# Loading and storing the first sixteen tokens of each partition in pieces of 1, 1, 2, 4 and 8

## The chip, the cores and the metric

The kernel runs on one core of one Trainium2 chip. The metric is the device time of one execution in microseconds. Six executions of the kernel before took 241.51 to 243.63 us, with a median of 242.13 us. One of them was recorded by the hardware profiler; all rows of a profile shown here come from such a recorded execution.

## The reference

The kernel is the dispatch step of a mixture of experts: each token's vector is written out once for each of its two experts, scaled by that expert's weight.

```
x:              16 x 1024 x 512   float32   (16384 tokens of 2 KB)
expert_weights: 16 x 1024 x 2     float32
out = x[:, :, None, :].repeat(2, axis=2) * expert_weights[..., None]
                16 x 1024 x 2 x 512 float32 (16384 tokens of 4 KB)
```

`expert_indices` is an input, but no value of it enters the result. So 33.6 MB of x are read, 0.13 MB of weights, and 67.1 MB are written; each element of x is multiplied twice.

## The kernel before

The 16384 tokens are laid over the 128 partitions of the on-chip memory so that partition p holds tokens 128p to 128p + 127. A partition's 128 tokens lie together in x (256 KB) and in the output (512 KB). `A_TOTAL` (line 25) is this 128. In what follows "16 tokens" always means 16 tokens of each partition.

The weights are loaded whole by one transfer on SyncE's (SP's) queue, line 45, into `w_tile`: 1 KB per partition. A loop of eight steps (line 47) then takes `TX = 16` tokens at a time. Line 49 loads them by one transfer on ScalarE's (ACT's) queue: 32 KB per partition, 4 MB in all. The pool of these tiles has two buffers, so loads 0 and 1 can be issued at once, and load 2 waits until VectorE is done with all of tile 0.

Within a step, an inner loop of two takes `TO = 8` tokens at a time. For each token and each of the two experts, VectorE (DVE) runs one multiply of 128 x 512 elements by a value per partition (line 59), 16 for an output tile. When the 16 are done, line 67 stores the tile by one transfer on SP's queue: again 32 KB per partition, 4 MB. The pool of output tiles has four buffers, so VectorE can be four tiles ahead of the stores at most, and its first multiply into a fifth waits for the first store to have landed.

Nothing plans or reorders this: each engine runs its instructions in the order written. ACT's queue holds only the eight loads, SP's the weights' load and the sixteen stores, VectorE's the 256 multiplies. The transfers of both queues run on the same 16 DMA engines. In the trace each transfer of a 128-partition tile is 128 packets, one per partition, eight on each engine; the packets of x and of the output are all 32 KB.

Of the kernel before, what the change touches and what calls it, by code (L numbers as in the profile page):

```python
# [1 line left out]

# [4 lines left out]


@with_exitstack
def kernel(  # L10
    ctx: ExitStack,
    tc: tile.TileContext,
    x: bass.AP,
    expert_indices: bass.AP,
    expert_weights: bass.AP,
    out: bass.AP,
):
    nc = tc.nc

    batch, seq, hidden = x.shape  # L20
    k = expert_weights.shape[-1]
    P = nc.NUM_PARTITIONS
    ntok = batch * seq
    assert ntok % P == 0
    A_TOTAL = ntok // P

    xr = x.rearrange("b s h -> (b s) h").rearrange("(p a) h -> p (a h)", a=A_TOTAL)
    outr = out.rearrange("b s k h -> (b s) (k h)").rearrange(
        "(p a) n -> p (a n)", a=A_TOTAL
    )  # L30
    wr = expert_weights.rearrange("b s k -> (b s) k").rearrange(
        "(p a) k -> p (a k)", a=A_TOTAL
    )
    f32 = mybir.dt.float32
    row = k * hidden

    TX = 16
    TO = 8

    w_pool = ctx.enter_context(tc.tile_pool(name="w_pool", bufs=1))  # L40
    x_pool = ctx.enter_context(tc.tile_pool(name="x_pool", bufs=2))
    o_pool = ctx.enter_context(tc.tile_pool(name="o_pool", bufs=4))

    w_tile = w_pool.tile([P, A_TOTAL * k], f32)
    nc.sync.dma_start(out=w_tile, in_=wr)

    for i in range(A_TOTAL // TX):
        x_tile = x_pool.tile([P, TX * hidden], f32)
        nc.scalar.dma_start(
            out=x_tile, in_=xr[:, i * TX * hidden : (i + 1) * TX * hidden]  # L50
        )
        for j in range(TX // TO):
            o_tile = o_pool.tile([P, TO * row], f32)
            for t in range(TO):
                at = (j * TO + t) * hidden
                for kk in range(k):
                    c = (i * TX + j * TO + t) * k + kk
                    o = t * row + kk * hidden
                    nc.vector.tensor_scalar(  # L59
                        out=o_tile[:, o : o + hidden],  # L60
                        in0=x_tile[:, at : at + hidden],
                        scalar1=w_tile[:, c : c + 1],
                        scalar2=None,
                        op0=mybir.AluOpType.mult,
                    )
            first = (i * TX + j * TO) * row
            nc.sync.dma_start(out=outr[:, first : first + TO * row], in_=o_tile)


# [1 line left out]
_INS = ['x', 'expert_indices', 'expert_weights']  # L71
_OUTS = [((16, 1024, 2, 512), 'float32')]


# [23 lines left out]
```

## Time and profile before

| what | value |
|---|---|
| median of six executions | 242.13 us |
| the profiled execution, its own time | 243.63 us |
| its span, first to last recorded event | 241.8 us |
| VectorE busy | 102.4 us (42%), 256 multiplies |
| read from and written to HBM | 33.69 MB and 67.11 MB, 417 GB/s over the span |
| stores: issue to landing, median of 16 | 44.9 us |
| loads of x: issue to landing, median of 8 | 24.6 us |
| load of the weights: issue to landing | 10.5 us |
| first multiply starts | 13.67 us |
| first store issued | 20.13 us |

Times within an execution count from the start of the span. The rows of digits divide the span into 40 equal slices of 6.05 us; a digit is the busy share of a slice in tenths, 9 standing for 90% or more. The row "DMA" is the mean busy share of the 16 DMA engines, the row below it what they moved. The queue named q1 is SP's and q10 is ACT's. Where the profile speaks of a releaser it means the event that ended a wait.

### The profile page before, as it was taken

How to read it: one execution, taken by the hardware profiler on the slowest of the kernel's cores; microseconds unless marked ns; L12 is line 12 of the kernel's file. 1: busy time of each engine (PE TensorE's matmuls, PEld its weight loads, DVE VectorE, ACT ScalarE, POOL GpSimd, SP SyncE). 2: the span in 40 equal slices, each digit the busy share in tenths (PEclk: the TensorE clock that was granted, in tenths of full speed). 3: DMA queues.
4: the chain of work that ended last, by engine and by line, in shares of the span. 5: the costliest groups of instructions: out<-in, count | busy, mean ns of one | idle time of the engine just before them, and what ended most of it. 6: DMA issues, size and time to landing. Idle time of an engine off the chain costs nothing.

```text
span 241.8 us, 358 instructions
## 1 busy us (share of the span) xinstructions
DVE 102.4 (42%) x256; POOL 0.2 (0%) x4
## 2 busy tenths in 40 slices
DVE  0079994039800904582073640649009295500000
POOL 0000000000000000000000000000000000000000
DMA  6999999999999999999999999999999999999993
GB/s 274 442 434 423 434 348 423 434 428 417 434 434 412 434 434 434 434 423 434 401 428 434 417 434 434 430 434 428 434 428 428 434 434 434 434 434 434 434 434 152
DMA packets 3602, 100.81 MB, mean 417 GB/s; under 512 B 400, under 2 KB 528, under 8 KB 528
## 3 DMA queue, kind: packets, MB, share of 16 engines
q1 hardware_dynamic: 2448, 67.24, 64.6%
q10 hardware_dynamic: 1152, 33.55, 33.4%
q14 instruction: 2, 0.02, 0.0%
HBM read 33.69 MB, written 67.11 MB: 417 GB/s over the span
## 4 chain that ended last, share of the span: by engine, by line
DMA 52%; DVE 21%; another core or an unknown queue 13%; issue 0%; DVEq 0%
DMA out_dram<-o_tile 36%; DVE o_tile L59 21%; DMA x_tile<-in_x_dram 16%; DVEq L93 0%; DVEq L59 0%
## 5 line engine op out<-in xcount | busy, mean ns | idle before, releaser
L59 DVE TENSOR_SCALAR o_tile<-x_tile,w_tile 128x512 f32<-128x512 f32 x256 | 102.4, 481 | 106.4 <-DMA out_dram<-o_tile 75.8
L82 POOL MEMSET const-bfloat16-1.0<- 128x1 bf16 x1 | 0.1, 102 | 0.0
L82 POOL MEMSET const-uint8-127<- 128x1 uint8 x1 | 0.1, 102 | 0.0
L82 POOL MEMSET const-float32-0.0<- 128x1 f32 x1 | 0.1, 99 | 0.2 <-issue 0.2
L82 POOL MEMSET const-float32-1.0<- 128x1 f32 x1 | 0.1, 99 | 0.0
## 6 DMA issues: line engine op xcount, KB each, us to landing
out_dram<-o_tile SPq DMA_DIRECT2D x16, 4096.0 KB, 44.9
x_tile<-in_x_dram ACTq DMA_DIRECT2D x8, 4096.0 KB, 24.6
w_tile<-in_expert_weights_dram SPq DMA_DIRECT2D x1, 128.0 KB, 10.5
```

Source lines behind the costliest of these rows:

```text
L59: nc.vector.tensor_scalar(out=o_tile[:, o : o + hidden], in0=x_tile[:, at : at + hidden], scalar1=w_tile[:, c : c + 1], scalar2=None, op0= ...
L82: nc = _bacc.Bacc("TRN2", target_bir_lowering=False, num_devices=1)
```

## The change

The first entry of a list of pieces, `[1, 1, 2, 4, 8]`, describes the first 16 tokens, and seven entries `[16]` describe the rest. A tile of x is loaded by one transfer per piece, and a store is issued whenever a piece ends or eight tokens are complete. So load 0 becomes five transfers, of 2, 2, 4, 8 and 16 KB per partition, all into one tile of x. The first output tile, tokens 0 to 7, leaves in four transfers, of 4, 4, 8 and 16 KB per partition; tokens 8 to 15 leave in one as before. Loads 1 to 7 and stores 1 to 15 keep their sizes, and so do the pools, the weights' load and the layout of tokens over partitions; the list `groups` has one group, which holds all 128 tokens of a partition. ACT's queue then has 12 loads, SP's the weights and 19 stores, VectorE the same 256 multiplies in the same order.

```diff
+    groups = [[[1, 1, 2, 4, 8], [16], [16], [16], [16], [16], [16], [16]]]
...
-    nc.sync.dma_start(out=w_tile, in_=wr)
+    def rows(of_all, done, T):
+        return of_all[done * P : (done + T) * P, :].rearrange(
+            "(p a) n -> p (a n)", a=T
+        )
...
+        nc.sync.dma_start(
+            out=w_tile[:, done * k : (done + T) * k], in_=rows(wf, done, T)
+        )
...
-        nc.scalar.dma_start(
-            out=x_tile, in_=xr[:, i * TX * hidden : (i + 1) * TX * hidden]
+        for pieces in group:
+            x_tile = x_pool.tile([P, TX * hidden], f32)
+            at = 0
+            for n in pieces:
+                nc.scalar.dma_start(
+                    out=x_tile[:, at * hidden : (at + n) * hidden],
+                    in_=xr[:, (a0 + at) * hidden : (a0 + at + n) * hidden],
+                )
+                at += n
+            ends = [sum(pieces[: i + 1]) for i in range(len(pieces))]
+            first = 0
+            for t in range(at):
+                if t % TO == 0:
+                    o_tile = o_pool.tile([P, TO * row], f32)
                 for kk in range(k):
-                    c = (i * TX + j * TO + t) * k + kk
-                    o = t * row + kk * hidden
+                    c = (done + a0 + t) * k + kk
+                    o = t % TO * row + kk * hidden
                     nc.vector.tensor_scalar(
...
-            first = (i * TX + j * TO) * row
-            nc.sync.dma_start(out=outr[:, first : first + TO * row], in_=o_tile)
+                if t + 1 in ends or (t + 1) % TO == 0:
+                    nc.sync.dma_start(
+                        out=outr[:, (a0 + first) * row : (a0 + t + 1) * row],
+                        in_=o_tile[:, first % TO * row : (t % TO + 1) * row],
+                    )
+                    first = t + 1
```

More of the change, by code (lines that the diff above doesn't have):

```diff
@@ L25 @@
     A_TOTAL = ntok // P
[L27 to L33, printed above, removed]
     f32 = mybir.dt.float32
@@ L38 @@
     TO = 8
+    groups = [[[1, 1, 2, 4, 8], [16], [16], [16], [16], [16], [16], [16]]]
+    assert sum(sum(sum(t) for t in g) for g in groups) == A_TOTAL
+    xf = x.rearrange("b s h -> (b s) h")
+    of = out.rearrange("b s k h -> (b s) (k h)")
+    wf = expert_weights.rearrange("b s k -> (b s) k")
     w_pool = ctx.enter_context(tc.tile_pool(name="w_pool", bufs=1))
@@ L44 @@
     w_tile = w_pool.tile([P, A_TOTAL * k], f32)
-    nc.sync.dma_start(out=w_tile, in_=wr)
-    for i in range(A_TOTAL // TX):
-        x_tile = x_pool.tile([P, TX * hidden], f32)
-        nc.scalar.dma_start(
-            out=x_tile, in_=xr[:, i * TX * hidden : (i + 1) * TX * hidden]
-        )
[L52 to L55, printed above, removed]
+    def rows(of_all, done, T):
+        return of_all[done * P : (done + T) * P, :].rearrange(
+            "(p a) n -> p (a n)", a=T
+        )
+    done = 0
+    for group in groups:
+        T = sum(sum(t) for t in group)
+        nc.sync.dma_start(
+            out=w_tile[:, done * k : (done + T) * k], in_=rows(wf, done, T)
+        )
+        done += T
+    done = 0
+    for group in groups:
+        T = sum(sum(t) for t in group)
+        xr = rows(xf, done, T)
+        outr = rows(of, done, T)
+        a0 = 0
+        for pieces in group:
[12 more added lines that the diff above has]
+                    o_tile = o_pool.tile([P, TO * row], f32)
                 for kk in range(k):
-                    c = (i * TX + j * TO + t) * k + kk
-                    o = t * row + kk * hidden
+                    c = (done + a0 + t) * k + kk
+                    o = t % TO * row + kk * hidden
                     nc.vector.tensor_scalar(
                         out=o_tile[:, o : o + hidden],
-                        in0=x_tile[:, at : at + hidden],
+                        in0=x_tile[:, t * hidden : (t + 1) * hidden],
                         scalar1=w_tile[:, c : c + 1],
@@ L65 @@
                     )
-            first = (i * TX + j * TO) * row
-            nc.sync.dma_start(out=outr[:, first : first + TO * row], in_=o_tile)
+                if t + 1 in ends or (t + 1) % TO == 0:
[4 more added lines that the diff above has]
+                    first = t + 1
+            a0 += at
+        done += T
 _INS = ['x', 'expert_indices', 'expert_weights']
```

## The prediction

> **What bounds the kernel now.** I read the page from the top: the busy shares and the 40 slices first, because they say which resource is never free, then the DMA queues, the chain of waits, and last a table of short windows around the stretch that the change touches.
>
> ```profile
> span 241.8 us, 358 instructions
> ...
> DVE 102.4 (42%) x256; POOL 0.2 (0%) x4
> ...
> DVE  0079994039800904582073640649009295500000
> ...
> DMA  6999999999999999999999999999999999999993
> GB/s 274 442 434 423 434 348 423 434 428 417 434 434 412 434 434 434 434 423 434 401 428 434 417 434 434 430 434 428 434 428 428 434 434 434 434 434 434 434 434 152
> ...
> q1 hardware_dynamic: 2448, 67.24, 64.6%
> q10 hardware_dynamic: 1152, 33.55, 33.4%
> ...
> HBM read 33.69 MB, written 67.11 MB: 417 GB/s over the span
> ```
>
> The DMA row is 9 in every slice but the first and the last: the 16 DMA engines have work from about 2 us to about 238 us. The queues of the stores (q1, with the weights) and of the loads (q10) take 64.6 + 33.4 = 98.0% of the engines' time. VectorE is busy for 42% and idles most of the rest. In the undisturbed slices the rate is 434 GB/s; 100.81 MB at that rate need 232.3 us, and the span is 241.8 us. So 9.5 us at most are there to be won by anything that doesn't cut bytes. They are made of: the head, about 2 us before data flows (packet records begin at 1.1 to 2.1 us, engine by engine); the end, about 4 us (the window 236 to 238 us still has a DMA share of 0.76, 238 to 240 us has 0.15, and the span runs to 241.8); and some 3.5 us in slices under 434, of which one slice, the sixth (30.2 to 36.3 us) at 348 GB/s, alone is 6.05 x (1 - 348/434) = 1.2 us.
>
> The chain of waits agrees: its greatest part is the store, its second VectorE waiting in turn for a buffer that a store must free.
>
> ```profile
> DMA 52%; DVE 21%; another core or an unknown queue 13%; issue 0%; DVEq 0%
> DMA out_dram<-o_tile 36%; DVE o_tile L59 21%; DMA x_tile<-in_x_dram 16%; DVEq L93 0%; DVEq L59 0%
> ```
>
> The table of waits gives us in total, times and longest:
>
> ```profile
> DVE o_tile L59 <- DMA out_dram<-o_tile: 75.8, 9, 12.7
> DVE o_tile L59 <- DMA x_tile<-in_x_dram: 27.2, 2, 13.7
> ```
>
> The 21% of VectorE in the chain does not set the end: while those multiplies run, the DMA row stays 9. The 13.7 us that VectorE waits for the first load look like the place where the change helps. Whether they do depends on what the DMA engines have to do meanwhile: columns here are the window's length, VectorE, GpSimd, PEclk, the DMA share and GB/s.
>
> ```profile
> 14.00:16.00 2.00, 2.00 (x6) 0.00 (x0) 1.00 0.87 377
> 16.00:18.00 2.00, 2.00 (x6) 0.00 (x0) 1.00 1.02 442
> 18.00:20.00 2.00, 2.00 (x6) 0.00 (x0) 1.00 1.14 492
> 20.00:22.00 2.00, 2.00 (x7) 0.00 (x0) 1.00 0.79 328
> 22.00:24.00 2.00, 2.00 (x7) 0.00 (x0) 1.00 1.07 459
> 24.00:26.00 2.00, 2.00 (x7) 0.00 (x0) 1.00 1.10 475
> ```
>
> A packet of 1.2 us is booked whole in one window, so single rows swing around 1; the six average 1.00. There is no gap between the loads and the first store. The two x buffers let loads 0 and 1 be issued at 0.73 us together; by the completion records load 1 leaves the engines at 21.3 to 22.8 us; the first store is issued at 20.13 us, so its packets are there in time. The DMA engines never waited for stores to begin.
>
> **The change, part by part.** Removed: no byte and no multiply.[...]
>
> Added on ACT's queue: 4 more loads. A load takes 366 ns there (the median of the eight). Load 1, the one behind them, is issued at 0.73 + 5 x 0.37 = 2.6 us in place of 1.1 us. By then the engines hold 4 MB of pieces, 9.7 us of work, which covers it. Without that cover it would cost 1.5 us. Piece 1 is 0.26 MB, 0.6 us of transfer, more than the 0.37 us until piece 2 is issued, so the queue does not run dry between pieces either.
>
> Added on SP's queue: 3 more stores at 333 ns each. SP has nothing between 1.1 and 20.1 us, so they cost nothing there.
>
> Added to the DMA engines: packets. The records show one packet per partition and transfer, 8 on each engine, plus one completion record of 9 ns. Loads: 4 x 8 = 32 more per engine; stores: the first 8-token store becomes four, 3 x 8 = 24 more. The 32 KB packets take 1213 ns (27.0 bytes a ns). No packet of 2, 4, 8 or 16 KB from the kernel is in the trace; the nearest below is the weights' 1 KB packet, median 46 ns, where 27 bytes a ns would make 38: 8 ns for being a packet. Its mean of 53 ns gives 15 ns. So 56 x 8 = 0.45 us on each engine, at most 56 x 15 = 0.84; I take 0.45, since the dear ones are the very first, and 7 x 9 ns = 0.06 us for completions. This falls on engines that are busy to the end, nothing hides it: **+0.5 us**.
>
> Here a rule of the Trainium skill speaks much louder against the change: DMA: Bandwidth & Descriptors, section "Bandwidth", asks for transfers of 1 MiB and more for 75% of peak, and its fit gives about 2.0 us fixed per DMA. By it 7 more DMAs cost 14 us and the kernel would take 256 us. The row says otherwise for DMAs that stand in a queue: between 212 and 236 us only stores run, several transfers one after the other, at a share of 100.5% and 434 GB/s. The fixed time is in the landing of each, and other packets fill it. I use the row, 0.5 us.
>
> Moved: VectorE's first multiply. It waits for piece 1 and the weights. The weights landed after 10.5 us because each of their 8 packets per engine alternated with one of 1213 ns; now they alternate with small ones, and both are through about 1 us after data begins to flow, near 4 us with the landing. At 399 ns a multiply (12.77 us for 32) store 1 is issued near 5.5 us in place of 20.1. The new waits on VectorE (one per piece in place of one) hold up its next multiplies, and through them SP's stores and ACT's load 2. The last piece of 8 tokens lands after 4.2 MB of loads and some 2 MB of stores, at about 15 us; its 16 multiplies end near 22 us, against 26.4 before. So load 2 comes some 4 us sooner, and nothing is later. None of it shortens the end, since the engines that carry it are full: by 22 us they have moved 8.7 MB out of 12.7 MB issued by then.
>
> Moved too: stores now run beside loads 0 and 1. Reads stretch when stores run beside them: q10's 33.4% is 80.8 us for 64 packets per engine, 77.6 us at 1213 ns, so 3.1 us lost, of which the packet records put only 0.2 us in the first two loads, which ran alone. That is 0.5 us for each of the six mixed loads. After the change about 1.2 loads more are mixed: 0.6 us, if the stretching goes by load; below nothing if it belongs to load 2's start alone (the 348 slice). Between 0.6 and -1.2 I take +0.3, nearer the mean row, since five other loads show some of it.
>
> Sum: 0.45 + 0.06 + 0.3 = 0.8 us. On the profiled execution, 243.63 us with a span of 241.8 and 1.8 us around it, that gives a span of 242.6 and 244.4 us. That execution is the longest of the six; on the median, 242.13, it gives **242.9 us**, +0.3%. A measurement of this kernel can tell about 0.5% (1.2 us) from no change, so I forecast no change that can be told.
>
> **The rivals.** (1) Slower: small packets are dearer than the weights' packet says. The weights' packets alternated with large ones; in the first 3 us after the change all packets on an engine are 1 to 4 KB, in step over 16 engines, at a row pitch of 256 KB. If packets of 2 and 4 KB move at half the rate, 1 MB of loads takes 2.4 us more; less what stores fill, 1.5. With 0.8 from packets and 0.6 from mixing the time is about 244.5 to 245. It decides from 0.7 us of such loss on. For it: the very first 32 KB reads took up to 1.76 us and one 1 KB packet 0.34 us. Against it: once flowing, the 1 KB packets held 46 ns steadily.
> (2) Faster: the 1.2 us lost in the sixth slice come from load 2's abrupt meeting with the first stores, and go when the two meet gradually; and the uneven end (share 0.76, then 0.15) happens to close up by a us. 242.1 + 0.5 - 1.2 - 1 = 240.4. Against it: loads 3 to 7 met stores that were already flowing, and still stretched.
> (3) The forecast that the words of the change suggest: stores begin 14 us sooner and so the end comes sooner, toward 228 us. The bytes exclude it: 232.3 us at 434 GB/s, before head and end.
> (4) The packets' cost vanishes among the ends of the engines, which differ by 2 us: 242.1.
>
> **How the numbers follow.** My sum 0.46, (4) 0.10: together 0.56 within 0.5% (240.9 to 243.3). (1) 0.32, all above 243.3. (2) 0.12, below 240.9, (3) under 0.01 in it. The range reaches from 241.2, which holds all but the lowest of (2), to 245.0, the upper end of (1).
>
> **What would show it.** Right: the DMA row still 9 from the second slice on; packets 896 more and 112 completion records, 4610 in all; the first store issued near 5.5 us; load 2 near 22 us; VectorE's wait for loads about as long in sum but in pieces, its wait for stores longer; the span within 1 us of 242.6. Wrong: a slice of the first 12 us clearly under 400 GB/s (rival 1), or the sixth at 434 and the last emptier (rival 2). A DMA digit under 9 in the middle would overthrow the bound on which all of this stands.

## The result: 0.2% faster, and the profile after

The changed kernel's median is 241.91 us (35 executions, 241.28 to 244.02), the kernel before has 242.53 us beside it (72 executions, 241.16 to 244.53). The ratio is 0.9979, 95% interval 0.9965 to 0.9993. So the change gains about 0.5 us. I had forecast 0.8 us of loss. Both are under the 0.5% that I had called the limit, and 241.91 lies in the range; but the sign was wrong, and the interval excludes no change. (A later, smaller comparison, e9_after_again below, has 0.9984 with an interval that just includes it.) The quickest executions of the two kernels are alike, 241.28 and 241.16 us. What differs is how many are quick: 23 of 35 are under 242.2 us after the change, 15 of 72 before.

The traced execution took 242.26 us, with a span of 240.5. These are the lines of its page that answer to those shown of before: the span, the slices, the packets and the queues.

```profile
span 240.5 us, 372 instructions
...
DVE  2558398460276404673054910917207495500000
...
DMA  6999999999999999999999999999999999999994
GB/s 190 401 458 412 447 435 406 458 431 436 431 431 420 425 431 436 436 425 431 436 431 436 431 436 425 432 431 431 431 431 436 436 431 436 431 431 436 436 425 185
DMA packets 4610, 100.81 MB, mean 419 GB/s; under 512 B 512, under 2 KB 640, under 8 KB 1280
...
q1 hardware_dynamic: 2880, 67.24, 65.1%
q10 hardware_dynamic: 1728, 33.56, 33.2%
```

The DMA row is still 9 in every slice but the first and the last, so the bound is what it was, and VectorE's row shows the early work (digits 2 and 5 in the first slices, where it had 0). The GB/s row holds the answer. The first slice fell from 274 to 190 and the second from 442 to 401; the sixth rose from 348 to 435. Slices are 6.0 us, so the first two lost (84 + 41) x 6.0 = 0.75 MB, 1.7 us at 434 GB/s, and the sixth regained 87 x 6.0 = 0.52 MB, 1.2 us. The rest is spread over the other slices: slices 7 to 39 have 430 GB/s on average before and 432 after.

The table of waits of the changed kernel, in us, times and longest:

```profile
DVE o_tile L83 <- DMA out_dram<-o_tile: 85.8, 11, 12.7
DVE o_tile L83 <- DMA x_tile<-in_x_dram: 15.1, 5, 5.0
DVE o_tile L83 <- issue: 3.8, 1, 3.8
```

VectorE waits 12 us less for loads (27.2 before) and 10 us more for stores (75.8): what it gains at the start it gives back to buffers that full DMA engines free no sooner.

**Where the time went, in the packet records.** In the kernel's transfers a packet of a given size has a steady time, its median; what single packets take above it I call stretching, summed and divided by the 16 engines. "Price" is all packets and completion records at their medians. The last store leaves a completion record on each engine; their mean is when the DMA engines are done on average, and the lag is how far the slowest is behind that. Times in this table, and wherever a mean end is given, put the first packet at 1.1 us; the profile's windows put it at 1.7 us, so these times are 0.6 us early against the windows. Two traces of each kernel (the second ones are the runs e1_before_again and e9_after_again below):

| trace, us per engine | price | stretching 0-8 us | 8-40 us | after 40 us | mean end | lag | span |
|---|---|---|---|---|---|---|---|
| before | 233.49 | 0.20 | 1.49 | 1.68 | 237.9 | 2.2 | 241.8 |
| before, second | 233.49 | 0.44 | 1.60 | 1.30 | 237.6 | 2.6 | 241.9 |
| changed | 234.02 | 1.58 | 0.04 | 0.64 | 236.9 | 1.7 | 240.5 |
| changed, second | 234.02 | 1.45 | 0.03 | 0.81 | 236.9 | 2.2 | 240.9 |

The packets cost 0.53 us more. The stretching falls from 3.35 to 2.28 us: 1.2 us more in the first 8 us, 1.5 less up to 40 us, 0.8 less after. Sum: -0.55 us. The mean end moved by 0.85, so 0.3 us (gaps of engines that start late, records that overlap by 3 to 4 ns) is not separated by this account. The lag is 0.45 us smaller. Together that is 1.3 us, which fits the spans (1.2 us) but is twice the difference of the medians: both traces of before are of executions from the upper part of its range (243.63 and 243.72 us), those of the changed kernel less so (242.26 and 242.66 us).

### The profile page after: what moved, and what is told of

Its sections match the earlier page's. It is cut to its first block, busy times and chain, and to the rows that moved or that the text cites. A ratio compares the mean times of both kernels' runs of the same rounds, so it can differ in the third digit from the quotient of the medians.

```text
span 240.5 us, 372 instructions
## 1 busy us (share of the span) xinstructions
DVE 102.9 (43%) x256; POOL 0.2 (0%) x4
## 2 busy tenths in 40 slices
DMA packets 4610, 100.81 MB, mean 419 GB/s; under 512 B 512, under 2 KB 640, under 8 KB 1280
## 4 chain that ended last, share of the span: by engine, by line
DMA 43%; DVE 23%; another core or an unknown queue 18%; issue 2%; DVEq 0%; ACTq 0%
DMA out_dram<-o_tile 32%; DVE o_tile L83 23%; DMA x_tile<-in_x_dram 11%; DVEq L123 0%; ACTq L70 0%; DVEq L83 0%
## 6 DMA issues: line engine op xcount, KB each, us to landing
out_dram<-o_tile SPq DMA_DIRECT2D x2, 512.0 KB, 16.4
```

## The experiments

Two theories stood at first. **M (meeting)**: before loses its 3 us because load 2 and the first stores start into each other, and an early store takes that away. **C (chance)**: the stretching comes and goes by itself. Before's own code ran again first; the other kernels are the changed one with a list of load pieces and a list of store pieces per tile that can differ:

```diff
-    groups = [[[1, 1, 2, 4, 8], [16], [16], [16], [16], [16], [16], [16]]]
-    assert sum(sum(sum(t) for t in g) for g in groups) == A_TOTAL
+    loads = ...
+    stores = ...
+    groups = [loads]
+    cuts = iter(stores)
...
-            ends = [sum(pieces[: i + 1]) for i in range(len(pieces))]
+            cut = next(cuts)
+            ends = [sum(cut[: i + 1]) for i in range(len(cut))]
```

### The kernel before, again

No edit.

> The kernel before, once more, timed against itself: it gives the error of a ratio and a second trace. Theory M (meeting): before loses about 2.9 us per engine to stretched 32 KB packets because load 2 and the first stores start into each other; the stretching is a property of the kernel, so the second trace again has 2.5 to 3.5 us of it and a slice under 400 GB/s between 24 and 40 us. Theory C (chance): the stretching comes and goes from execution to execution; the second trace has anything from 0.5 to 3 us, and no slice need be low. Both: ratio 1.000, interval within 0.998 to 1.002.

Median 242.56 us against 242.71, ratio 0.9991 (0.9963 to 1.0019). The stretching was 3.34 us in place of 3.37, in the same places. The transfers of the window from 26 to 38 us, first in the trace of before, then in this one (kind: packets, MB, share of 16 engines):

```profile
DMA packets 155, 4.56 MB, mean 380 GB/s; under 512 B 15, under 2 KB 15, under 8 KB 15
...
q1 hardware_dynamic: 106, 2.98, 59.3%
q10 hardware_dynamic: 48, 1.57, 40.3%
```

```profile
DMA packets 156, 4.56 MB, mean 380 GB/s; under 512 B 16, under 2 KB 16, under 8 KB 16
...
q1 hardware_dynamic: 105, 2.92, 59.2%
q10 hardware_dynamic: 50, 1.64, 41.3%
```

40.3% of 12 us on 16 engines is 77.4 us for 48 read packets, 1.61 us each where 1.21 is the steady time; 41.3% for 50 gives 1.59. Two traces with the same stretching in the same places speak against C: it seems to belong to the kernel. But they are only two, and both of long executions, so they do not exclude C. The same window of the changed kernel, in both its traces:

```profile
DMA packets 292, 5.36 MB, mean 446 GB/s; under 512 B 32, under 2 KB 32, under 8 KB 34
```

```profile
DMA packets 288, 5.30 MB, mean 441 GB/s; under 512 B 27, under 2 KB 27, under 8 KB 30
```

The 380 GB/s of before are 446 and 441 there (over 434, since a packet is booked whole where it starts).

### One part of the change at a time

Only the loads cut, then only the stores:

```diff
+    loads = [[1, 1, 2, 4, 8], [16], [16], [16], [16], [16], [16], [16]]
+    stores = [[8, 8], [8, 8], [8, 8], [8, 8], [8, 8], [8, 8], [8, 8], [8, 8]]
```

> Only the first load is cut in 1, 1, 2, 4, 8; the stores stay at 8 tokens. The first store is issued near 11 to 14 us, while load 1 is under way. M: the stretching later on goes (-2.4 us), the slow start of the small load packets stays (+1.6), packets +0.3: -0.5 us, ratio 0.998, as in the changed kernel. C: the later stretching is unrelated, slow start and packets alone: +0.3 to +1.9 us, ratio 1.001 to 1.008.

```diff
+    loads = [[16], [16], [16], [16], [16], [16], [16], [16]]
+    stores = [[1, 1, 2, 4, 8], [8, 8], [8, 8], [8, 8], [8, 8], [8, 8], [8, 8], [8, 8]]
```

> Only the first stores are cut in 1, 1, 2, 4, 8; load 0 is one transfer of 16 tokens. The first store is issued near 14.5 us in place of 20.1. M: no slow start, the later stretching goes: -2.4 + 0.2 = -2.2 us, ratio 0.991. C: +0.2 us for packets, ratio 1.001.

Loads cut: median 244.31 us, ratio 1.0066 (1.0042 to 1.0090). Stores cut: 243.20, ratio 1.0014 (0.9995 to 1.0032). M had put them at 0.998 and 0.991; both fit what C had put (1.001 to 1.008, and 1.001). Neither half of the change gains; only the two together do. With the stores cut, the stretching that should have gone had moved: none in load 2, but 1.18 us in load 1, at 19 to 22 us, while the first small stores run beside it. So cutting the stores does not make the meeting gentle. (The profile's windows put this at 19 to 23 us.)

### The first load in two halves

```diff
+    loads = [[8, 8], [16], [16], [16], [16], [16], [16], [16]]
+    stores = [[8, 8], [8, 8], [8, 8], [8, 8], [8, 8], [8, 8], [8, 8], [8, 8]]
```

> The first load in two halves of 8 tokens (16 KB packets), stores as before. The first half lands near 8 us, the first store is issued near 14 us. No packet under 16 KB but the weights'. M: no slow start, later stretching goes: -2.3 us, ratio 0.990. C: +0.1 us, ratio 1.000.

Median 241.68 us, ratio 0.9952 (0.9929 to 0.9975): half of what M said. Here the burst moved into load 1, to 15 to 18.5 us. The first store is issued at 14.85 us, but its first packet starts at 19.2 us. The window from 13 to 19 us:

```profile
DMA packets 64, 2.10 MB, mean 350 GB/s; under 512 B 0, under 2 KB 0, under 8 KB 0
...
q10 hardware_dynamic: 64, 2.10, 95.1%
```

64 packets take 91.3 us, 1.43 us each, and no store packet is among them: these reads were stretched while no store moved at all. What is gone is the later stretching: 0.48 us after 40 us in place of 1.68.

M falls in its form. Stretching in the first 40 us is 1.3 to 2.1 us in all traces up to here and in the three kernels of the next two sections, wherever the cut is. So the greater part of the gain comes from what follows 40 us. New theories: **S (start)**: small load packets are stretched only where they are the first on engines that set off in step, and time is price plus stretching plus the lag of the slowest engine. **P (packets)**: small load packets are stretched wherever they stand.

### The same pieces, elsewhere

In reverse order:

```diff
+    loads = [[8, 4, 2, 1, 1], [16], [16], [16], [16], [16], [16], [16]]
+    stores = [[8, 4, 2, 1, 1], [8, 8], [8, 8], [8, 8], [8, 8], [8, 8], [8, 8], [8, 8]]
```

> The same pieces in the order 8, 4, 2, 1, 1, so the same packets, but the small ones stand behind 8 tokens and the first store (8 tokens) is issued near 15 us. Two theories. S (start): small load packets are stretched only where they are the first on engines that set off in step; behind 8 tokens they run at their price (84 to 311 ns), stretching before 12 us under 0.5 us per engine, one burst of about 1 us where stores first join load 1; as with two halves plus 0.45 us for packets: -0.7 us, ratio 0.997. P (packets): small load packets are stretched wherever they stand; 1.2 us per engine between 6 and 12 us; ratio 1.002.

Median 243.00 us, ratio 1.0021 (0.9989 to 1.0053). The small load packets ran at full rate: the window from 8 to 12 us of this kernel, and then the window from 2 to 8 us of the changed kernel and of before.

```profile
DMA packets 384, 1.67 MB, mean 418 GB/s; under 512 B 38, under 2 KB 38, under 8 KB 270
...
q10 hardware_dynamic: 384, 1.67, 101.0%
```

```profile
DMA packets 632, 1.80 MB, mean 299 GB/s; under 512 B 64, under 2 KB 170, under 8 KB 554
...
q10 hardware_dynamic: 510, 1.69, 92.1%
q1 hardware_dynamic: 122, 0.11, 6.1%
```

```profile
DMA packets 161, 2.55 MB, mean 424 GB/s; under 512 B 0, under 2 KB 86, under 8 KB 86
```

418 GB/s with packets of 2 to 8 KB behind a large piece, 299 with the same packets at the start (q1's 0.11 MB there are the weights; the first store packet starts at 8.9 us): P is wrong, and S right in that small load packets are stretched near the start and not behind. (Stretching before 12 us is 0.6 us per engine, over the 0.5 that S had put, but none of it is in the small load packets.) But S's reason does not fit the single packets. The first ones on the engines, of 2 KB, took 92 and 89 ns on average in the two traces, where 84 is the median; those of the third and fourth piece were stretched, between 3.7 and 9.8 us: 4 KB 242 and 188 ns (median 159), 8 KB 387 and 423 ns (median 309). S's time was wrong too (0.997), since the stretching after 40 us is 1.68 us here, as in before. The packets are the same and the late gain is gone, in this one trace and in the median; that points to the order and not to the packets.

The pieces in tokens 16 to 31:

```diff
+    loads = [[16], [1, 1, 2, 4, 8], [16], [16], [16], [16], [16], [16]]
+    stores = [[8, 8], [1, 1, 2, 4, 8], [8, 8], [8, 8], [8, 8], [8, 8], [8, 8], [8, 8]]
```

> Pieces 1, 1, 2, 4, 8 for tokens 16 to 31 in place of 0 to 15, loads and stores; the first load is whole and the first store is issued near 20 us as in the kernel before. S: the small packets run unstretched at about 12 to 14 us; load 2 keeps its burst of over 1 us near 30 us: +0.5 us, ratio 1.002. P: 1.2 us more at 12 to 16 us: +1.7 us, ratio 1.007.

Median 243.02 us, ratio 1.0001 (0.9957 to 1.0045). No stretching at 12 to 16 us: P is wrong again. A burst of about 0.9 us between 28 and 35 us remained, as S said, and 0.88 us came after 40 us.

### All tiles in pieces

```diff
+    loads = [[1, 1, 2, 4, 8], [1, 1, 2, 4, 8], ...]
+    stores = [[1, 1, 2, 4, 8], [1, 1, 2, 4, 8], ...]
```

> All eight tiles loaded and stored in pieces 1, 1, 2, 4, 8: 8 x 56 = 448 more packets per engine than the kernel before and 56 completion records. S: 448 x 8 ns + 56 x 9 ns = 4.1 us more, less up to 1 us of stretching that goes: +3 to +4 us, ratio 1.013 to 1.017. P: every set of small load packets loses 1.2 us: +10 us and more, ratio above 1.04.

Median 246.64 us against 242.77: 3.9 us more, ratio 1.0157 (1.0097 to 1.0217). Its page:

```profile
span 245.0 us, 448 instructions
...
DMA packets 11667, 100.82 MB, mean 412 GB/s; under 512 B 1296, under 2 KB 1424, under 8 KB 6544
```

The price of its packets is 237.77 us, 4.28 over before. S is met. Its small load packets (2 to 8 KB) were stretched by 1.35 us per engine in the first tile and by 0.36 us in the other seven together. This run measures the packet price, magnified eightfold. It also decides against adding 2.0 us for each DMA here, where DMAs stand in a queue: 56 more would have cost 112 us.

### Loads cut: why slower?

> Only the first load cut, once more, for a second trace (the first trace fell on its fastest execution, 243.16 us where the median was 244.31). Where do the 1.6 us come from that it lost to the kernel before? S: the mean end of the 16 engines is near 236.5 us as in the first trace, and the slowest engine is 4 us or more behind it. P: the mean end itself is near 238 us, with 1 to 2 us more stretching.

One execution, 243.24 us: mean end 237.0, lag 2.5, stretching 2.36. It again was a quick one and shows no 4 us of lag. Inconclusive, so the kernel ran once more below, beside the changed one and the two halves on another chip. There, theory **K (chip)** was that such differences belong to the chip.

> The changed kernel once more, beside the two that differ most, on one chip. Theory S (sum over the engines: packet price, stretching, and how far the slowest engine lags): stretching again 1.2 to 1.8 us in the first 8 us, under 0.3 us from 8 to 40 us, 0.4 to 0.9 us later; ratio 0.996 to 1.000. Theory K (chip): differences of half a per cent between these kernels belong to the chip they ran on; on another chip the order of the changed kernel, loads cut and two halves need not be the same.

> Only the first load cut. S: slower again by 0.4 to 0.9%, the slowest engine 3 us or more behind the mean; so the cut stores, not the cut loads, carry the gain of the whole change. K: about the changed kernel's time, ratio 0.997 to 1.002.

> The first load in two halves, once more. S: ratio 0.993 to 0.997 again, stretching 1.3 to 1.8 us up to 40 us and about 0.5 later. K: ratio 0.998 to 1.002.

The changed kernel: 241.93 us, ratio 0.9984 (0.9963 to 1.0005). Loads cut: 244.21, ratio 1.0060 (1.0034 to 1.0086). Two halves: 242.29, ratio 0.9979 (0.9957 to 1.0000). Loads cut is slower by about 0.6% on both chips, so K is wrong for it. The two halves gained less than S had said and stand level with the changed kernel: 0.9979 is nearer to K's 0.998 to 1.002 than to S's 0.993 to 0.997, so K stays open for them. The trace of loads cut is now of an execution of 245.04 us. The end of its span, then the same windows of the changed kernel's second trace (length, VectorE, GpSimd, PEclk, DMA share, GB/s):

```profile
236.00:238.00 2.00, 0.00 (x0) 0.00 (x0) 1.00 0.68 295
238.00:240.00 2.00, 0.00 (x0) 0.00 (x0) 1.00 0.08 33
240.00:242.00 2.00, 0.00 (x0) 0.00 (x0) 1.00 0.04 16
```

```profile
236.00:238.00 2.00, 0.00 (x0) 0.00 (x0) 1.00 0.50 213
238.00:240.00 2.00, 0.00 (x0) 0.00 (x0) 1.00 0.04 16
240.00:242.00 2.00, 0.00 (x0) 0.00 (x0) 1.00 0.00 0
```

In the first, a share of 0.04, one packet of 1.2 us among 16 engines, starts past 240 us: the mean end is 237.7, the slowest engine 3.6 us behind. In the second they are 236.9 and 2.2. So of the 2.4 us between the two spans (243.3 and 240.9) the lag is 1.4, the mean end 0.8; the latter is stretching, 3.1 us against 2.3. S's figure for the lag, 3 us or more, is met in this trace; the two quick ones have 3.0 and 2.5 us, not the 4 that S had put for the second. The three traces, on three chips, also show how far executions of one kernel differ: stretching of 1.9, 2.4 and 3.1 us, of it 0.37, 0.55 and 1.18 us after 40 us. What makes one engine fall behind when only the loads are cut stays open.

### Every load in halves

```diff
+    loads = [[8, 8], [8, 8], [8, 8], [8, 8], [8, 8], [8, 8], [8, 8], [8, 8]]
+    stores = [[8, 8], [8, 8], [8, 8], [8, 8], [8, 8], [8, 8], [8, 8], [8, 8]]
```

> Every load in two halves of 8 tokens (16 KB packets), stores as in the kernel before. Per engine 64 more packets at 2 x 611 - 1213 = 9 ns and 8 completion records: +0.6 us. S: gains no stretching over two halves in the first load alone, since later loads there are stretched by only 0.5 us in sum: 0.5 us slower than that, ratio 0.996 to 0.999. Against S: if 16 KB packets are stretched less wherever reads join stores, up to 0.5 us faster than S says, ratio 0.994 or less.

A miss for every theory: six executions took 248.47 to 262.09 us, median 257.56, where before has a median of 242.70. The quickest is 2.4% above that, the other five about 6% and more. The traced one is the longest, so what follows tells of it and not of the quickest. Its slices and waits ("issue" is a wait whose end the profile does not name):

```profile
GB/s 262 441 390 427 431 425 446 403 441 408 425 441 395 431 418 443 400 428 431 398 428 410 423 415 433 403 429 410 390 433 420 451 415 312 400 285 267 408 55 20
...
DVE o_tile L86 <- issue: 90.6, 9, 10.8
DVE o_tile L86 <- DMA x_tile<-in_x_dram: 43.8, 5, 10.3
```

The rate holds until slice 33 and then breaks (312, 285, 267), with 55 and 20 in the last two slices. The completion records show why: the 16 engines finish the half that ends near 31 us within 1.7 us of each other, and the one near 150 us within 14.7 us. The slowest falls behind step by step, and at the end the others have nothing left while it works on: mean end 248.3 us, lag 10.2. Stretched store packets go with it, 3.6 us per engine on average after 40 us where before has 0.14. The price of its packets is only 0.65 us above before. The records do not name the engine of a packet, so that the stretched stores are those of the lagging engines is likely, not shown; why they are stretched on and on was not found.

## Why the prediction was wrong

**The bound was right.** The DMA engines stay full from the second slice on, no gap was there for early stores to fill, and no time of the order of the 15 us by which the first store moved was gained. It was issued at 4.72 us (forecast 5.5), load 2 at 23.23 us (forecast 22), 4610 packets are as counted. Rival 3, an end that follows the first store, is out.

**The cost of packets was right.** Forecast 0.45 + 0.06; at the measured medians of 84, 159, 309 and 611 ns for 2, 4, 8 and 16 KB it is 0.53 us. With the pieces in all tiles the same price predicted 4.1 us and 3.9 were measured. The row was the better guide than the 2.0 us per DMA of the Trainium skill's page DMA: Bandwidth & Descriptors, by which the changed kernel would have taken 256 us. That fit stands in the page's section "Anatomy of one DMA — SWDGE (gpsimd) path", not in "Bandwidth" as I had it, and is for DMAs issued from GpSimd; those here are issued from SP and ACT, and I had not said so.

**The issue on ACT's queue was right in its effect, not in its course.** I had load 1 issued at 2.6 us. The loads of the first 6 us, from the list of line 70 (count: minimum, median and maximum ns, first and last start in us):

```profile
L70 ACTq DMA_DIRECT2D x_tile<-in_x_dram x6: 335/454/471, 0.7 to 4.4; - x6
```

The last of them, load 1, starts at 4.4 us: it waits on the semaphore that the second piece's landing counts up, as its issue record shows, and so for that landing. I had not named that wait. The cover held: the last packets of load 0 leave the engines at 14.8 to 16.4 us, and load 1's first one starts at 14.8 us.

The packet times in the prediction (1.1 to 2.1 us for the first, 21.3 to 22.8 us for the end of load 1) are 0.6 us early against the profile's windows. No term of the sum hangs on them.

**The step that failed is the stretching of reads ("Moved too").** I took +0.3 us from between +0.6 and -1.2. It measured -1.1 us in the traces (3.35 to 2.28), near the other end, and that turns the sign: 0.5 - 1.1 = -0.6. That the medians differ by the same 0.6 us is partly luck: in the same traces the lag adds 0.45 us and 0.3 us are not separated, and their spans differ by 1.2 us. Both signs of being wrong that I had named came true at once. A first slice clearly under 400 was rival 1's, and its loss is there: 1.2 us more at the start, close to the 1.5 I had priced. Its form was another: I had put it on packets of 2 and 4 KB in the first 3 us, and it fell on those of 4 and 8 KB, mostly from 4 to 8 us. The sixth slice at 435 was rival 2's, and its gain is there: 1.2 us by the slice, 1.5 by the records. I had treated as alternatives what were two terms of one sum, and added neither.

Why I chose wrongly: I argued that reads stretch when stores run beside them, so more mixing means more. Two things in the traces contradict it. Reads are stretched with no store beside them: the 1.2 us at the start of the changed kernel before its first store packet at 8.9 us, the burst of the two halves before 19.2 us. And after the change more reads run beside stores and fewer of them are stretched: after 40 us 0.32 and 0.53 us per engine of read packets against 1.54 and 1.21 before, for somewhat fewer bytes (21 MB against 23 MB between 40 and 200 us). Two traces of each kernel agree. The argument against rival 2, that loads 3 to 7 also stretch, was no argument: theirs fell too.

**What is shown and what is not.** Shown: in the first 40 us the stretching is moved by the order of the pieces and hardly removed (1.3 to 2.1 us); small load packets are stretched almost only near the start; reads are stretched without stores too. In the single traces, the later part (1.68 and 1.30 us in before) is 0.48 to 0.88 us in the changed kernel, with the pieces in tokens 16 to 31, with stores cut and with halves, 0.37, 0.55 and 1.18 us with loads cut, and 1.68 and 1.84 us with the same pieces reversed or in all tiles. The account has a limit: single executions of one kernel differ by 2 to 3 us and a trace shows one of them. The total stretching of before, of the changed kernel and of the halves agrees within 0.3 us between two traces, but the three of loads cut differ by 1.2 us, as much as before and the changed kernel do. Both traces of before are from the upper part of its range, so that some of the 1.1 us may be theirs and not the change's: the change may as well have made quick executions more frequent as each one quicker, and no trace of a quick execution of before was taken. Theory C is not excluded for this part. Stores cut shows how little one trace says of a median: 0.24 us more price and 0.8 us less stretching than in before's traces, a span 0.5 us shorter, and a median 0.5 us longer. Not shown: that the fall in stretching is what lowers the median; what in the memory or the engines stretches a read, and why the order of the first 40 us still counts after 100 us. The lag of the slowest engine, 1.1 to 3.6 us in these kernels apart from the last one, is a term that I had only as an "uneven end" in a rival; it is as large as the terms I priced, and it is the greater part of what makes loads cut slow in the trace of 245.04 us.

## What to carry to other kernels

Where the DMA engines are busy from end to end, starting stores sooner moves work about and takes none away; the gain or loss is in packet price and in how smoothly reads and writes mix, -0.5% to +0.7% here for cuts of one tile. Read the GB/s row slice by slice before pricing such a change, and add up what each low slice may give and what each new small packet may take, in place of letting them compete. Two halves in place of five pieces did as well; but don't cut on in the same direction without a run: with halves in every tile the quickest of six executions took 2.4% longer, the others 6% and more.

## What the runs showed of the hardware that I had not expected

- In the window 2 to 8 us, small load packets moved at 299 and 309 GB/s, the ones of 4 and 8 KB being stretched; the same packets behind 2 MB of larger ones moved at 418.
- A burst of stretched reads, mostly 0.5 to 1.3 us per engine, appears within the first 40 us in every kernel: near the start where the pieces begin small, in load 1 with halves, with the order reversed and with stores cut, in load 2 in the kernel before. Loads cut has a second burst in two of its three traces. With small pieces at the start, with halves and with the order reversed, the burst is over, but for some hundredths of a us, before the first store packet moves.
- A transfer can wait long for its first packet though nothing of its own queue is ahead of it: the first store of the changed kernel was issued at 4.7 us and moved its first packet at 8.9 us, that of the two halves at 14.9 and 19.2 us.
- The 16 DMA engines can drift apart. Each has its fixed eight packets of every transfer, so an engine that falls behind is not helped by the others: the lag at the end is 1.1 to 3.6 us here, and 10.2 us in the longest execution with all loads in halves.
- Loads cut, whose price is 0.2 us under that of the changed kernel, has a median 2.3 us above it on the same chip.
